# Moving all SSM input products, the second gates and the second time step into the first stage of a conv–Mamba block

## The chip, the cores and the metric

The kernel runs on one core of a Trainium2 chip. The metric is device time in microseconds (us) for one execution of the whole program. Of the kernel before there are three timed runs, and one profiled execution whose trace is read here. The engines are named as in the profile: PE multiplies matrices, DVE, ACT and POOL work on rows of 128 partitions, and SP issues the DMA transfers, in order, from one queue.

## The reference, cut to what matters

One block works on 1024 tokens of width 1024, all in fp32. Cut to the lines that the change touches or that stand beside it:

```
shift, scale, gate = adaln(c, w_ada_mix, b_ada_mix)        # mod = silu(c) @ w + b, 3 x 1024
h    = rms_norm(x, norm_mix_w) * (1 + scale) + shift
proj = h @ w_in
conv_in, z, xbc, dt_raw, g_conv, g_ssm = split(proj, [2048, 2048, 3072, 32, 1024, 1024])
u      = a_half * sigmoid(b_half)                           # conv_in
u      = silu(layer_norm(causal_depthwise_conv31(u)))       # mean and variance over 1024 channels
y_conv = u @ w_conv_out
xbc    = silu(causal_depthwise_conv4(xbc))                  # xs: 2048, B: 512, C: 512 channels
dt     = softplus(dt_raw + dt_bias)
y      = ssd_chunked_scan(xs, dt, -exp(a_log), B, C) + d_skip * xs
y      = group_rms_norm(y * silu(z)) * ssm_norm_w           # 4 groups of 512 channels
y_ssm  = y @ w_ssm_out
x      = x + gate * ((sigmoid(g_conv) * y_conv + sigmoid(g_ssm) * y_ssm) @ w_out)
# then a SwiGLU FFN with its own adaln (w_ada_ffn), and a final rms_norm
```

## The kernel before, in words

The activations stand transposed: 128 channels on the partitions, 512 tokens along the row. The 1024 tokens are two halves of 512 (`hf` 0 and 1), and a width of 1024 is eight such tiles. Every fp32 value that PE multiplies is split into a rounded part and a rest (`h` and `l` in the names), and one product of a 128x128 weight block with a 128x512 tile is three matmuls: high by high, high by low, low by high. All of these are called wide matmuls below.

There are two ways to compute a product of `h` with columns of `w_in`. A plain one, `mm3` (L177), takes one 128-column chunk and one half of the tokens: eight blocks by three matmuls, 24 wide matmuls. It needs the whole chunk split (128x1024, `split_w_`, L163 on ACT and L164 on DVE), and it needs that again for the other half. The other way is a unit (`Unit`, L904), which takes two chunks and both halves at once and uses a scheme of seven block products in place of eight: 7 x 12 = 84 wide matmuls where four plain products take 96. A unit combines quarters of the raw weights (L928 to L937), splits seven sums of them (`wsplit`, L795 and L796), and leaves its results in three PSUM tiles, uX, uY and uZ. Its operands for the second half are differences of the two halves' tiles, T1 to T4 and B22, made once by `tok_ops`.

**First stage** (`phase_a`). After the first norm and six plain gate products (`gate0`), 27 units run, one every 84 matmuls: eight for `conv_in`, eight for z, five for the gates and six (`SsmIn`) for the SSM inputs of groups 0 and 3 (`G_BOTH`). The list `CI_AT` and the insertions by `G_AT` and `G_STEP` set their order. The width-4 convolution of an SSM chunk follows inside its unit, in two halves of 512 tokens, with three more small instructions for the seam (L1131). From the fifth unit on POOL makes the weight sums and splits (`ENG_A`). Background generators are drained by `tick` at a set number of steps per 12 matmuls (`set_drains`): here the width-31 convolution (`conv31`, 47 steps on DVE for each 128 channels), its mean (`conv_mean`), the variance of the first half (`conv_var(0)`), and the time step of the first half (`dt_part`).

**Second stage** (`phase_b`). Plain products follow for groups 1 and 2, half by half: `group` with `conv4`, 24 chunk halves, and `gates1`, six products of the second half. `next_h` makes the normed second half for them from x (it is written to `O`). Beside these run the products with `w_conv_out` (`conv_out`), `w_ssm_out` (`smul`) and `w_out` (`wout`), 1536 wide matmuls together. In the background run the scan (`ssd_all`, which waits for `ready` and for the time step), the second half's time step, `conv_norm` and `conv_var(1)`, and the modulations: `ada` multiplies 128x512 pieces of `w_ada_mix` and `w_ada_ffn` with silu(c) on DVE (L249).

The scan takes eight groups in a row, (half, g). One group turns B over (`bT`, L510), makes C·B (`cb`) and the masked `cbm`, turns the inputs over (`xT`), makes the four chunk states (`st`, L536), and then for four pairs of heads loads rows of the decays from DRAM (M, L547, and E, L603), lets ACT and DVE make M of them, multiplies (`yo`, L608, and `yd`, L623) and gates with z (`y`, L629). `ssd_norm` then sends a row of group norms through DRAM (`bcy`), scales y (L652) and stores it. The y tiles are a ring of four, the M tiles too. `ysplit` loads y back as an operand of `smul` and waits for its group.

**Third stage**: the FFN (`ffn_in`, `down_both`, `down_rest`), which the change leaves alone.

The order on each engine is not the written one. The framework orders the instructions of every engine by a model of their times, under the dependences and with a preference for weight loads (`PRI_W`). Each engine then runs its list in order, so that an instruction which waits holds up those behind it; that is true of SP's list too.

## Time and profile before

| | |
|---|---|
| three timed runs, median (lowest to highest) | 2091.88 us (2086.75 to 2101.56) |
| the profiled execution: its own time | 2084.13 us |
| its span, first to last instruction | 2082.4 us |
| busy: PE, DVE, ACT, POOL | 1941.3, 1574.0, 1004.0, 646.8 us |
| moved by DMA | 366.43 MB, mean 176 GB/s |

The profile lists busy time per engine and per group of instructions; a line such as L164 is a line of the kernel before. A matmul that is followed at once by another counts from its start to its modelled end, so the sum over single matmuls is larger than the time that they take up. A group's row gives its count, its busy time and the mean of one instruction, and then the idle time of the engine just before these instructions and what ended it. A row by window gives for a stretch of time each engine's busy time and count, the granted PE clock, the share of the 16 DMA engines and the GB/s.

### The profile page before, as it was taken

To read this page: it belongs to the slowest core of one execution; us is meant where nothing else is said; L and a number is where in the kernel's file an instruction comes from. 1 tells how busy PE (TensorE), PEld (TensorE's weight loads), DVE (VectorE), ACT (ScalarE), POOL (GpSimd) and SP (SyncE) were. 2 spreads that over 40 slices of the span, in tenths; PEclk is the share of its full clock that TensorE was granted. 3 is DMA by queue.
4 is the path that set the end of the run, shared out by engine and by line. 5 is a ranking of instruction groups with operands and counts; after the bars stand their busy time and mean duration, and the time that the engine had idled before them with its cause. 6 is when DMAs were issued, how large, how long until landed. Compare 5 with 4: busy or idle time off the path is not lost.

```text
span 2082.4 us, 26179 instructions
## 1 busy us (share of the span) xinstructions
PE 1941.3 (93%) x8802; PEld 1548.7 (74%) x8802; DVE 1574.0 (76%) x2458; ACT 1004.0 (48%) x1938; POOL 646.8 (31%) x487
## 2 busy tenths in 40 slices
PE   4899899999998899998899999998999999989997
PEld 3788688887876677776677777776888888767876
DVE  8878989878797978989797965759543443699655
ACT  4644454443444867566555733335333333444243
POOL 0008688888870000100000000005443443331400
...
GB/s 348 86 105 93 76 97 102 116 86 107 104 86 215 271 198 237 243 294 304 266 315 264 239 247 245 250 241 64 154 81 86 85 73 101 186 244 234 202 174 119
DMA packets 163958, 366.43 MB, mean 176 GB/s; under 512 B 18744, under 2 KB 19184, under 8 KB 163824
## 3 DMA queue, kind: packets, MB, share of 16 engines
...
q14 instruction: 65, 0.53, 0.1%
...
## 4 chain that ended last, share of the span: by engine, by line
PE 59%; DVE 20%; DMA 12%; issue 4%; ACT 3%; POOL 1%; SPq 0%; DVEq 0%; ACTq 0%; POOLq 0%
PE uXp L817 10%; PE uXf L817 10%; PE uZp L817 5%; PE uZf L817 5%; PE uXd L817 3%; PE uYp L817 2%; PE uYf L817 2%; DMA M<-acs_d 2%; PE s L189 2%; PE s L187 2%; PE s L188 2%; DMA E<-eac_d 2%; DMA wa_f<-in 1%; DVE gc L1128 1%; DMA wa_m<-in 1%
## 5 line engine op out<-in xcount | busy, mean ns | idle before, releaser
L163 ACT ACTIVATE wh<-w 128x1024 fp32r<-128x1024 f32 (+1 forms) x110 | 113.4, 1032 | 108.6 <-PE s L188 37.4
L164 DVE TENSOR_TENSOR wl<-w,wh 128x1024 fp32r<-128x1024 f32 (+1 forms) x110 | 130.7, 1189 | 23.3 <-ACT wh L163 15.8
L531 POOL TENSOR_TENSOR S<-S,dt_etot 128x512 f32<-128x512 f32 x16 | 20.5, 1281 | 294.7 <-ACT S L538 138.5
L557 ACT ACTIVATE M<-M,dt_acs 128x128 f32<-128x128 f32 x256 | 80.0, 394 | 59.4 <-DMA M<-acs_d 58.6
L930 POOL TENSOR_TENSOR fw<-fw,fw 128x512 f32<-128x512 f32 x37 | 59.5, 1608 | 120.2 <-DMA fw<-in 118.6
L672 DVE SCALAR_TENSOR_TENSOR pcM<-u,cw_eo,pcM 128x512 f32<-128x512 f32 x120 | 90.2, 752 | 2.5
L672 DVE SCALAR_TENSOR_TENSOR pcQ<-u,pc,pcQ 128x512 f32<-128x512 f32 x112 | 84.3, 753 | 2.7
L187 PE MATMUL s<-Hh,wh 128*128 128x512 f32 x192 | 76.4, 402 | 6.3 <-ACT Hh L217 4.0
L672 DVE SCALAR_TENSOR_TENSOR pcR<-u,pc,pcR 128x512 f32<-128x512 f32 x104 | 78.4, 754 | 2.7
L189 PE MATMUL s<-Hh,wl 128*128 128x512 f32 x192 | 76.8, 400 | 3.6 <-DVE wl L164 3.6
L187 PE MATMUL p<-Hh,wh 128*128 128x512 f32 x144 | 62.3, 453 | 18.0 <-DVE xo L1109 9.0
L188 PE MATMUL s<-Hl,wh 128*128 128x512 f32 x192 | 77.1, 402 | 0.9 <-DVE Hl L218 0.8
L845 POOL TENSOR_TENSOR b<-Hh,Hl 128x512 f32<-128x512 f32 x4 | 5.9, 1480 | 223.3 <-DVE spare L329 211.9
L817 PE MATMUL uXp<-T2h,dp 128*128 128x512 f32 x216 | 72.0, 395 | 3.0 <-ACT dp L795 3.0
L817 PE MATMUL uZp<-B22h,ep 128*128 128x512 f32 x216 | 72.4, 397 | 2.2 <-POOL ep L796 1.6
L817 PE MATMUL uYp<-Hh,bp 128*128 128x512 f32 x216 | 72.8, 399 | 1.0 <-DVE s1g L997 1.0
L817 PE MATMUL uXp<-T3h,fp 128*128 128x512 f32 x216 | 72.0, 396 | 1.2 <-ACT s L985 0.9
L817 PE MATMUL uXp<-T4h,gp 128*128 128x512 f32 x216 | 72.5, 396 | 0.4 <-DVE s5c L997 0.4
L817 PE MATMUL uZp<-T1h,cp 128*128 128x512 f32 x216 | 72.0, 395 | 0.0
L817 PE MATMUL uXp<-Hh,ap 128*128 128x512 f32 x216 | 71.0, 390 | 0.0
L188 PE MATMUL p<-Hl,wh 128*128 128x512 f32 x144 | 61.3, 427 | 5.4 <-DVE Hl L346 5.4
L817 PE MATMUL uZf<-T1h,cf 128*128 128x512 f32 x176 | 59.4, 401 | 3.5 <-DVE g L997 3.5
...
## 6 DMA issues: line engine op xcount, KB each, us to landing
fw<-in SPq DMA_DIRECT2D x134, 512.0 KB, 3.3
w<-in SPq DMA_DIRECT2D x100, 512.0 KB, 5.1
...
```

What stands on the lines that cost most here:

```text
L163: act(out=hi, in_=w[:, :nk * P], func=AF.Copy)
L164: eng.tensor_tensor(out=lo, in0=w[:, :nk * P], in1=hi.bitcast(F32), op=ALU.subtract)
L187: nc.tensor.matmul(out=out, lhsT=whi[:, sl], rhs=rh, start=first and i == 0, stop=False)
L188: nc.tensor.matmul(out=out, lhsT=whi[:, sl], rhs=rl, start=False, stop=False)
L189: nc.tensor.matmul(out=out, lhsT=wlo[:, sl], rhs=rh, start=False, stop=last and i == n - 1)
L531: gp.tensor_tensor(out=v3(sn), in0=v3(S[c]), in1=heads(etot, c, g), op=ALU.mult)
L557: act(out=m[:, sl], in_=m[:, sl], func=AF.Relu, scale=-1.0, bias=acs[:, c * 32 + hd:c * 32 + hd + 1])
L672: vec.scalar_tensor_tensor(out=pt if k < n - 1 else out or pt, in0=src(k), scalar=w(k), in1=pt, op0=ALU.mult, op1=ALU.add)
L817: nc.tensor.matmul(out=out, lhsT=l[:, sl], rhs=r, start=first and k == 0 and i == 0, stop=k == 3 and i == 2, skip_group_check=True)
L845: gp.tensor_tensor(out=t, in0=H[k][0].bitcast(F32), in1=H[k][1].bitcast(F32), op=ALU.add)
L930: e[8].tensor_tensor(out=a21, in0=a11, in1=a21, op=ALU.subtract)
L1128: vec.scalar_tensor_tensor(out=t[:, d:], in0=src[:, :T - d], scalar=wc(k), in1=t[:, d:], op0=ALU.mult, op1=ALU.add)
```

## The change

All twelve `SsmIn` units (four groups) now stand in the first stage, which has 33 units in place of 27; `S_AT` lists their places. The width-4 convolution runs over both halves at once, on rows of 1024 tokens, when both are there, so the seam's small instructions go and three DVE instructions per chunk are left; `conv4`, `group`, `next_h` for the second half and the list `ready` are gone. The second half of the six first gates (`gates1`, 24 matmuls each) becomes `gate1` and `half_b`, placed after the units in `GATE_AT`, with 24 matmuls each on the operands B22 and T3 that the units have already. The time step of the second half is made in the same way from those operands (`dt_part(1)`, started by `conv_mean`). The variance of the second half (`conv_var(1)`) and nearly all the modulations (`ada_bg`) are drained in the first stage too. The last two units of the first stage are kept for the end (`A_TAIL`), and ahead of them `tail` starts the layer norm of the first half, `conv_norm(0, H)`.

The second stage starts the scan at once and has only `conv_out`, `smul` and `wout` beside it, in a new order (both halves of `conv_out` first). The scan's input tiles get twice the buffers (`N_BC`, `N_XS`), and a group's inputs are loaded while the group before is at step `SSD_AHEAD`. In all there are 72 wide matmuls fewer, and 30 fewer splits of whole weight chunks.

```
-G_BOTH = (0, 3)
-G_AT, G_STEP = 3, 4
+A_TAIL = 2
+S_AT = (4, 7, 10, 13, 15, 17, 20, 23, 25, 27, 29, 31)
+GATE_AT = (5, 8, 11, 14, 18, 21)
-CONV_RATE = 2.2
+CONV_RATE = 2.4
-SSD_RATE = 0.85
+SSD_RATE = 1.2
-ADA_RATE = 0.6
-MEAN_WAIT = 10
+ADA_RATE = 0.75
+N_BC, N_XS = 4, 8
+SSD_AHEAD = 16
+MEAN_WAIT = 24
+N_EV = 4
...
+    def half_b(out, raw, name):
+        a, b = raw
+        s = pools["u"].tile([P, T], F32, tag="fs", name="fs" + name, bufs=pools["nfs"])
+        gp.tensor_tensor(out=s, in0=a, in1=b, op=ALU.add)
+        mmp(out, wsplit(s, "s" + name, vec), BO["B22"])
+        t = w2("n" + name)
+        hi, lo = t[:, 0:4 * P], t[:, 4 * P:]
+        act(out=hi, in_=a, func=AF.Copy, scale=-1.0)
+        vec.scalar_tensor_tensor(out=lo, in0=a, scalar=-1.0, in1=hi.bitcast(F32), op0=ALU.mult, op1=ALU.subtract)
+        mmp(out, (hi, lo), BO["T3"], False)
...
             if self.i == KD - 1:
-                bg_conv_a.extend([conv_mean(), conv_var(0)])
+                bg_conv_a.extend([conv_mean(), conv_var(0), conv_var(1)])
...
     class SsmIn(Sums):
-        def conv(self, src, m, hf, before=None):
+        def conv(self, src, m):
...
-            t = mp.tile([P, T], F32, tag="x0", name=f"gc{hf}_{i}", bufs=2)
+            t = mp.tile([P, 2 * T], F32, tag="x2", name=f"gc{i}", bufs=2)
             act(out=t, in_=src, func=AF.Identity, scale=wc(SW - 1), bias=sb_h[:, i:i + 1])
             for k in range(SW - 1):
                 d = SW - 1 - k
-                vec.scalar_tensor_tensor(out=t[:, d:], in0=src[:, :T - d], scalar=wc(k), in1=t[:, d:],
+                vec.scalar_tensor_tensor(out=t[:, d:], in0=src[:, :2 * T - d], scalar=wc(k), in1=t[:, d:],
                                          op0=ALU.mult, op1=ALU.add)
-                if before is not None:
-                    vec.scalar_tensor_tensor(out=t[:, :d], in0=before[:, T - d:], scalar=wc(k), in1=t[:, :d],
-                                             op0=ALU.mult, op1=ALU.add)
...
+        def tail(_):
+            finish(bg_dt)
+            bg_conv_a.append(conv_norm(0, H))
...
-        for n, (g, q) in enumerate((g, q) for g in (1, 2) for q in range(6)):
-            group(0, g, H, [q])
-            if 0 <= n - NH_AT < KD:
-                next_h(n - NH_AT, O, r_x[1], "x1m", lambda k: xT[1, :, k, :], gmix, mod_m)
-        step(spares)
-        conv_to(0, H)
-        gates1()
-        group(1, 1, O)
         step(lambda _: conv_done(0))
         many(lambda m: conv_out(0, m, H), range(KD))
+        step(lambda _: conv_done(1))
+        many(lambda m: conv_out(1, m, O), range(6))
         ysplit(0, 0, H)
-        group(1, 2, O)
+        many(lambda m: conv_out(1, m, O), range(6, KD))
         many(lambda m: smul(0, 0, m, H, None), range(KD))
```

How the lists of the engines change is shown at three places. The first is DVE's list in the first stage, where an SSM unit has its convolution. `gc` is the convolution's result, `gx` and `s` are the two halves of its input before (`gx` holds both after), `pcR` and `pcQ` are running sums of the width-31 convolution, and `s1z` and `gy` are results of units. Before:

```order
L1128 SCALAR_TENSOR_TENSOR gc_16_1621<-s_1601,pc,gc_16_1621 128x509
L1131 SCALAR_TENSOR_TENSOR gc_16_1621<-gx_1367,pc,gc_16_1621 128x3
L672 SCALAR_TENSOR_TENSOR pcR_1521<-u_1219,pc,pcR_1521 128x512
L997 TENSOR_TENSOR s_1581<-s_1581,uXp_1350 128x512
L1128 SCALAR_TENSOR_TENSOR gc_16_1621<-s_1601,pc,gc_16_1621 128x510
L1131 SCALAR_TENSOR_TENSOR gc_16_1621<-gx_1367,pc,gc_16_1621 128x2
```

And now, later in the same stage; `ud` and `sav` belong to a variance, `wa_f` and `gffn` to the modulations:

```order
L1151 SCALAR_TENSOR_TENSOR gc_5572<-gx_5292,pc,gc_5572 128x1021
L1032 TENSOR_TENSOR gy_5519<-gy_5519,uXp_5272 128x512
L332 TENSOR_TENSOR sav_5464<-sav_5464,sqv_3_5549 128x512
L1151 SCALAR_TENSOR_TENSOR gc_5572<-gx_5292,pc,gc_5572 128x1022
L744 TENSOR_TENSOR ud_4_5553<-ud_4_5553,bcmean_5440 128x512
L1151 SCALAR_TENSOR_TENSOR gc_5572<-gx_5292,pc,gc_5572 128x1023
L252 ISA wa_f_01_5557,gffn<-wa_f_01_5557,rw,as_f_0_5555 128x512
```

The convolution's instructions are twice as long and have no seam, and variances and modulations stand between them which came in the second stage before.

The second place is PE's list where the first stage ends. `uXp` is the last unit, `p_10` the first plain product of group 1, `co_0` the first product with `w_conv_out`, whose operands H are the layer norm's output. Before:

```order
L817 MATMUL uXp_4784<-T4h_1039,gp_5058 128x512
L188 MATMUL p_10_5138<-Hl_116,wh_5130 128x512
L189 MATMUL p_10_5138<-Hh_115,wl_5131 128x512
L187 MATMUL p_10_5138<-Hh_117,wh_5130 128x512
L188 MATMUL p_10_5138<-Hl_118,wh_5130 128x512
```

And now:

```order
L191 MATMUL co_0_6595<-Hl_112,wh_6587 128x512
L192 MATMUL co_0_6595<-Hh_111,wl_6588 128x512
L190 MATMUL co_0_6595<-Hh_113,wh_6587 128x512
L191 MATMUL co_0_6595<-Hl_114,wh_6587 128x512
L192 MATMUL co_0_6595<-Hh_113,wl_6588 128x512
L840 MATMUL uXp_6128<-T4h_1022,gp_6536 128x512
L840 MATMUL uXp_6128<-T4l_1023,gp_6536 128x512
```

Six of the eight tiles of the layer norm are now used before the last block product of the last unit.

The third place is PE's list inside the first group of the scan; `p_20` is a plain product of group 2, `S` the chunk states, `wx` and `btok` what they are made of, `bc` the tile of C. Before:

```order
L187 MATMUL p_20_5692<-Hh_117,wh_5609 128x512
L536 MATMUL st_5381<-wx_5339,btok_5177 128x512
L292 MATMUL bx1m<-ident,r_x_129 4x128
L188 MATMUL p_20_5692<-Hl_118,wh_5609 128x512
L189 MATMUL p_20_5692<-Hh_117,wl_5610 128x512
L608 MATMUL yo_5458<-bc_20_5156,S_5250 128x128
L608 MATMUL yo_5458<-bc_20_5156,S_5321 128x128
L536 MATMUL st_5462<-wx_5384,btok_5177 128x512
```

And now:

```order
L551 MATMUL st_6798<-wx_6745,btok_6630 128x512
L623 MATMUL yo_6840<-bc_20_6601,S_6694 128x128
L623 MATMUL yo_6840<-bc_20_6601,S_6725 128x128
L190 MATMUL co_5_7085<-Hh_117,wh_6996 128x512
L191 MATMUL co_5_7085<-Hl_118,wh_6996 128x512
L192 MATMUL co_5_7085<-Hh_117,wl_6997 128x512
L551 MATMUL st_6844<-wx_6801,btok_6630 128x512
```

The filler between the scan's steps is now products with `w_conv_out`, no longer products whose result needs a convolution. Counted in wide matmuls without the states, PE's list has 2407 from the first `uXp` to the first `bT`, 1435 from there to the last `yd` of the scan, 730 from there to the first matmul of the FFN and 2808 after it; now these are 3034, 968, 498 and 2808. Between the same two ends of the scan SP's list had transfers of 141 MB, counted from the first `xs` to the last E, and now has 104 MB.

213 lines of the change are left out of this document (94 added, 119 removed).

## The prediction

> **What bounds the kernel now.** I read the page first, then busy time by window over the four stretches that the order of PE's work gives, then the scan group by group, and last DVE's groups of instructions in two of the stretches. In the page's first part stand busy time, share of the span and count per engine:
>
> ```profile
> span 2082.4 us, 26179 instructions
> PE 1941.3 (93%) x8802; PEld 1548.7 (74%) x8802; DVE 1574.0 (76%) x2458; ACT 1004.0 (48%) x1938; POOL 646.8 (31%) x487
> ```
>
> PE is busy nearly throughout, but an average over stages hides where it runs freely and where it is held up. The next rows are windows: the start, the first stage up to the first step of the scan (`bT`), a piece of that stage, the scan up to the last group's end, the rest of the second stage, and the FFN. Columns: length, then busy time of PE, PEld, DVE, ACT and POOL with counts, the granted PE clock, the DMA share, GB/s.
>
> ```profile
> 0.00:65.80 65.80, 35.43 (x129) 26.86 (x129) 54.04 (x110) 34.09 (x55) 1.60 (x10) 0.95 0.78 289
> 65.80:669.80 604.00, 578.49 (x2473) 463.38 (x2474) 519.37 (x731) 278.10 (x469) 384.20 (x301) 0.98 0.31 104
> 300.00:400.00 100.00, 99.64 (x431) 80.52 (x430) 94.22 (x124) 44.52 (x76) 84.51 (x68) 1.00 0.30 103
> 669.80:1209.00 539.20, 493.50 (x2597) 383.12 (x2596) 465.08 (x847) 352.43 (x866) 31.15 (x32) 0.96 0.82 263
> 1209.00:1384.70 175.70, 170.93 (x728) 137.79 (x728) 108.90 (x176) 60.12 (x82) 1.29 (x1) 0.98 0.73 242
> 1384.70:2082.40 697.70, 662.90 (x2881) 537.57 (x2879) 426.63 (x595) 279.26 (x467) 228.54 (x143) 0.98 0.43 143
> ```
>
> In the middle of the first stage (300 to 400) PE has no gap: 431 matmuls in 100 us, 0.232 us each, although DVE is busy 94% and POOL 85%. So there PE is the bound, and a busy DVE does not hold it up. During the scan it is otherwise. PE is busy 91.5% (493.5 of 539.2), at a lower clock, and its list has only 1435 wide matmuls, 333 us at 0.232, beside the scan's own small ones. These are the eight groups of the scan, from one `bT` to the next:
>
> ```profile
> 669.81:731.44 61.63, 52.41 (x279) 40.68 (x278) 54.09 (x84) 50.71 (x134) 3.68 (x8) 0.92 0.85 278
> 731.44:836.36 104.92, 98.50 (x476) 74.34 (x474) 87.06 (x176) 70.11 (x159) 3.37 (x6) 0.95 0.70 216
> 836.36:888.93 52.57, 52.57 (x282) 41.46 (x281) 47.36 (x88) 30.72 (x86) 5.41 (x3) 1.00 0.79 255
> 888.93:978.51 89.58, 81.49 (x417) 63.99 (x417) 78.34 (x143) 59.94 (x146) 5.39 (x4) 0.96 0.89 293
> 978.51:1022.54 44.03, 42.27 (x256) 33.69 (x254) 35.26 (x77) 22.60 (x61) 3.13 (x3) 1.00 0.76 254
> 1022.54:1076.50 53.96, 45.10 (x245) 33.29 (x245) 45.62 (x84) 35.32 (x96) 3.13 (x3) 0.94 0.96 317
> 1076.50:1146.95 70.45, 65.95 (x350) 52.15 (x349) 59.51 (x104) 38.36 (x91) 4.58 (x3) 0.98 0.88 279
> 1146.95:1209.00 62.05, 55.19 (x302) 43.52 (x301) 57.84 (x98) 44.68 (x100) 2.48 (x2) 0.95 0.74 235
> ```
>
> A group's length follows the work put beside it: 44 us where that is least, 105 us where it is most. DVE is busy 80 to 93% of each group and close to PE in all. The two together set the pace, and what stands beside the scan decides how long it takes.
>
> **The change, part by part.** The start and the FFN keep their lists: 65.8 us and 697.7 us stay.
>
> *First stage.* Its list grows from 2407 to 3034 wide matmuls, by 627: six units of 84, the gates' 144, the time step's 24 and 22 of `conv_out` come in, 67 of plain products go. At 0.232 us (the row 300 to 400) that is 145.5 us, and the stage goes from 604.0 to 749.5 us if PE stays the bound. DVE's part has to be shown to fit. These rows are the width-4 convolution (L1128, and the seam L1131) between 65.8 and 580, and then L1128 after 612, with shortest, median and longest:
>
> ```profile
> L1128 DVE SCALAR_TENSOR_TENSOR gc<-s,pc,gc 128x509 f32<-128x509 f32 (+2 forms) x21 | 22.4, 1066 | 0.0
> L1128 DVE SCALAR_TENSOR_TENSOR gc<-gx,pc,gc 128x509 f32<-128x509 f32 (+2 forms) x12 | 15.8, 1317 | 1.0 <-ACT gc L1125 0.9
> L1131 DVE SCALAR_TENSOR_TENSOR gc<-gx,pc,gc 128x3 f32<-128x3 f32 (+2 forms) x12 | 10.6, 885 | 0.0
> L1128 DVE SCALAR_TENSOR_TENSOR gc<-gy,pc,gc 128x509 f32<-128x509 f32 (+2 forms) x9 | 8.9, 991 | 0.0
> L1131 DVE SCALAR_TENSOR_TENSOR gc<-gy,pc,gc 128x3 f32<-128x3 f32 (+2 forms) x9 | 4.0, 439 | 0.0
> ...
> L1128 DVE SCALAR_TENSOR_TENSOR gc<-s,pc,gc x12: 737/741/751, 614.5 to 656.5; 128x509 f32<-128x509 f32 x4, 128x510 f32<-128x510 f32 x4, 128x511 f32<-128x511 f32 x4
> ```
>
> And two rows of the scan's window, where POOL is all but idle, the split of a whole weight chunk and a modulation piece:
>
> ```profile
> L164 DVE TENSOR_TENSOR wl<-w,wh 128x1024 fp32r<-128x1024 f32 x60 | 74.0, 1234 | 8.3 <-ACT wh L163 8.3
> ...
> L249 DVE CUSTOM_DVE_ANT_0 wa_f<-wa_f,rw,as_f 128x512 f32<-128x512 f32 x16 | 12.4, 778 | 5.2 <-DMA wa_f<-in 5.2
> ```
>
> After 612 one instruction takes 0.741 us; while POOL splits weights it takes 1.12 us (47.1 over 42). Even the seam's rows of one to three elements mean 0.885 us. So what is lost beside POOL looks like a wait per instruction, 0.38 us on these, not a slower pace. The new instructions have twice the length. None is in this trace; the nearest is the 1024-wide two-input split, L164, at 1.234 us. With one wait of 0.38 that is 1.61 us, and 72 of them 116 us; without any wait they cost 89 us, and stretched in proportion (1.12 over 0.741) 134 us. I take 116, for the short rows' sake.
>
> The Trainium skill (SBUF — State Buffer, section "Who interferes with whom") says that a DVE instruction with two SBUF inputs and a POOL instruction that reads SBUF exclude each other for the whole instruction, and that the later one is blocked, not slowed. The short rows agree. By that rule the 116 us stand; by a shared bandwidth it would be the 134.
>
> The old convolution cost 61.7 us in the five rows up to 580, and some 22 more until 670 (ten of the 24 chunk halves at three times 0.741), so the new one adds 32 us. With the other work that comes in, DVE gains: 18 additions of unit results at about 0.7, 12; 48 modulation pieces at 0.778 (L249) and a wait of 0.38, 56; parts of the variances, 19 at 0.7, 13; three quarters of one layer norm, 18 at 0.7, 13; twelve gate splits, 9; a second time step, 15 by my estimate from some 20 instructions of 0.7; and it loses about 15 of plain products. Together 135 us: 654 of 749.5, 87%, where it has 86% now and bears 94% in the row 300 to 400 with PE full. POOL gains 72 instructions at 1.24 (84.51 over 68), 89 us: 63%, as now. For longer waits of SP behind the convolution's stores, and for the end, where the layer norm has to be ready before PE's last unit is through, I add 5 us, between 0 and 40. The cover of all this is PE's list; what it costs without it is the second rival.
>
> *The scan.* It loses 467 wide matmuls beside it, 108.3 us at 0.232; of PE's 493.5 us 385.2 are left. On DVE these rows of the scan's window matter too:
>
> ```profile
> L1106 DVE SCALAR_TENSOR_TENSOR p<-pre,pc,p 128x512 f32<-128x512 f32 x63 | 46.8, 750 | 0.3 <-ACT p L1102 0.2
> ...
> L652 DVE SCALAR_TENSOR_TENSOR y<-y,pc,bcy 128x512 f32<-128x512 f32 x28 | 19.2, 748 | 6.6 <-DMA bcy<-row_d 6.6
> ...
> L1109 DVE SCALAR_TENSOR_TENSOR xo<-pre,p 128x512 f32<-128x512 f32 x22 | 15.0, 682 | 4.2 <-DMA xbc_d<-xo 2.5 <-ACT pre L1108 1.6
> ...
> L746 DVE SCALAR_TENSOR_TENSOR un<-lnt,un 128x512 f32<-128x512 f32 x16 | 11.4, 715 | 0.9 <-ACT lnt L741 0.9
> ...
> L721 DVE TENSOR_TENSOR ud<-ud,bcmean 128x512 f32<-128x512 f32 x10 | 6.8, 687 | 2.0 <-DMA ud<-uc_d 2.0
> ```
>
> `conv4` goes (46.8 + 15.0), 19 of 60 weight splits (19 x 1.234 = 23.4), all 48 modulation pieces that ran here (48 x 0.778 = 37.3), 30 of 48 layer norm steps (21.5), the variance (6.8), and `next_h` (16 at 0.75, 12.0). That is 162.8; 13 more pieces of `conv_out` and y splits come in (8.9). DVE keeps 311 of 465 us. At the fullest group's share (57.84 of 62.05, 93%) it needs 334 us, at today's 86% 361. ACT's 352 us now are below that before anything is taken off. SP's list carries 104 MB in place of 141, which over 393 us is the 263 GB/s of now, within 1%. So PE is the later one: 385 us, at the share it has in the two groups with little DVE work (52.57 of 52.57 and 42.27 of 44.03, 98% in the mean) 393 us, 49 a group. At today's 91.5% it is 421; with a full clock and no gap 370 (385 x 0.96). I take 393, by those two groups, since these have what all have now: products and scan, little beside. The waits that go are those of `group` for its convolution; what is late next is a pair of M tiles or the y ring.
>
> *The rest of the second stage.* It has 498 wide matmuls in place of 730; at 175.7/730 = 0.241 us each, 119.9 us.
>
> The sum is 65.8 + 749.5 + 5 + 393 + 119.9 + 697.7 = 2030.9 us, and with the 1.7 us between span and time 2032.6 against the profiled 2084.1, 2.5% less. The median of the three runs lies 0.37% above the profiled one; I carry that over: 2040 us against 2091.9. Of the 51.5 us, 72 x 0.232 = 16.7 are fewer matmuls and the rest is the scan no longer held up.
>
> **The rivals.**
>
> *The scan's own chain sets the pace.* A group must load M and E, pass them through ACT and DVE, norm its y by way of DRAM and give its y tiles back before the next group can load z into them. For it: on ACT these waits are the largest of the scan,
>
> ```profile
> ACT M L557 <- DMA M<-acs_d: 58.6, 27, 6.7
> ```
>
> in total, times and longest; L652 waits 6.6 us for `bcy`; and groups one and eight take 61.63 and 62.05 us with only 52 to 55 us of PE work. If each group takes 62 us whatever stands beside it, the scan takes 496, and the time is 2136 by the profile, 2143 by the median. Against it: one group went through in 44.03 us and two more in under 54. It makes the kernel slower from 55.6 us a group on, (393 + 51.5)/8, and by over 1% from 58.2.
>
> *DVE holds up the longer first stage.* If it can't pass today's 86% there and its convolution stretches in proportion, 672 us of work (654 + 18) need 781: 32 us more, in place of the 5 counted, so 2060, or 2067 by the median. With a layer norm that is late at the end as well (40 us) it is 2100 by the profile. For it: its list now has the variances, which go through DRAM twice, among 27 to 33 units. Against it: the row 300 to 400.
>
> *The scan keeps PE's share.* If its gaps come from the scan and not from `conv4`, 385.2/0.915 = 421: 2061, or 2068 by the median, and with a few us more in the first stage no change that can be told.
>
> *Better than forecast.* With PE's clock full throughout the scan, 370, and nothing lost at the end of the first stage, 2005 by the profile, 2012 by the median; with the scan at DVE's 361, 1996 and 2003.
>
> **How the numbers follow.** About 1% is what a measurement of this kernel can tell from no change: 2071 to 2113. The forecast (2012 to 2062 by the median) gets 0.53, the better case 0.13, the scan at PE's present share 0.11, DVE in the first stage 0.09, the scan's chain 0.14. The predicted time is 2040. The range goes from 1996, a little below the better case's 2003, to 2100, which takes in the second and third rival and both together (27 + 28 us on 2040, 2095); it leaves out most of the slow case. Faster by over 1%: the forecast and the better case, 0.66. Within 1%: the second and third rival, 0.20. Slower: the scan's chain, 0.14.
>
> **What would show it.** The first stage is right if the last `uXp` ends near 740 to 790 us with PE at 0.232 us a matmul in mid-stage, and wrong if PE's waits there name DVE or ACT for tens of us. The price of the long convolution: a mean near 1.6 us for the 1021- to 1023-wide rows; 1.9 speaks for a stretch. The scan: eight groups between 44 and 54 us each, first `bT` to last `yd` about 393 us, PE over 95% busy. If groups take 60 us with PE under 85% and the waits name M, `bcy` or y, the first rival is right. The whole is wrong if the FFN's 697.7 us change, since nothing in it does.

## The result and the profile after

The changed kernel takes 2102.9 us in the median of 20 runs (2092.3 to 2119.7), the kernel before on the same chips 2089.4 (2084.9 to 2101.6). The ratio is 1.0063, with a 95% interval of 1.0042 to 1.0083: slower by 0.6%, where 2.5% less was forecast. The profiled execution took 2103.7 us, close to the median.

The first part of its page shows PE with 4.5 us less to do than before, in a span that is 19.3 us longer:

```profile
span 2101.7 us, 25836 instructions
PE 1936.8 (92%) x8729; PEld 1541.7 (73%) x8729; DVE 1551.6 (74%) x2312; ACT 993.3 (47%) x1885; POOL 777.9 (37%) x547
```

The next rows are the windows of the prediction: start, first stage up to the first `bT`, a piece of that stage, scan, rest of the second stage, FFN (columns as there).

```profile
0.00:68.80 68.80, 36.12 (x128) 27.52 (x128) 59.16 (x126) 34.34 (x55) 1.53 (x8) 0.90 0.83 308
68.80:850.70 781.90, 738.54 (x3161) 589.12 (x3161) 659.64 (x906) 370.91 (x594) 514.55 (x371) 0.97 0.39 129
300.00:400.00 100.00, 98.82 (x430) 80.07 (x429) 90.34 (x111) 42.25 (x70) 86.36 (x66) 1.00 0.29 93
850.70:1268.00 417.30, 376.27 (x2059) 290.80 (x2058) 314.63 (x536) 262.63 (x704) 29.66 (x24) 0.94 0.77 250
1268.00:1403.00 135.00, 122.46 (x507) 95.70 (x506) 90.12 (x152) 46.02 (x66) 1.29 (x1) 0.95 0.72 242
1403.00:2101.70 698.70, 663.39 (x2881) 538.53 (x2879) 428.03 (x595) 279.44 (x467) 230.91 (x143) 0.98 0.43 143
```

Against the forecast's 2030.9 us the difference of 70.8 lies so: start +3.0, first stage +27.4 (781.9 against 749.5 + 5), scan +24.3 (417.3 against 393), rest +15.1 (135.0 against 119.9), FFN +1.0. The middle of the first stage (300 to 400) runs as freely as before.

The eight groups of the scan, `bT` to `bT`, the last to its last `yd`:

```profile
850.69:898.65 47.96, 47.96 (x259) 37.48 (x257) 36.30 (x54) 36.46 (x95) 3.52 (x3) 1.00 0.97 336
898.65:950.88 52.23, 44.34 (x230) 32.73 (x229) 33.98 (x62) 30.72 (x88) 3.54 (x3) 0.87 0.63 199
950.88:1000.29 49.41, 43.63 (x250) 34.08 (x250) 39.71 (x69) 32.20 (x92) 4.33 (x3) 0.93 0.80 266
1000.29:1051.72 51.43, 45.29 (x234) 34.08 (x233) 34.05 (x60) 33.14 (x92) 5.11 (x4) 0.93 0.68 218
1051.72:1100.26 48.54, 39.99 (x232) 31.32 (x231) 34.95 (x63) 31.45 (x87) 3.13 (x3) 0.83 0.88 281
1100.26:1165.69 65.43, 59.26 (x304) 46.19 (x303) 53.61 (x89) 34.71 (x84) 4.82 (x3) 0.97 0.77 243
1165.69:1221.72 56.03, 52.52 (x288) 40.64 (x287) 44.16 (x75) 34.06 (x90) 3.13 (x3) 0.97 0.81 262
1221.72:1268.00 46.28, 43.27 (x269) 34.28 (x269) 37.87 (x72) 29.90 (x80) 2.09 (x2) 1.00 0.63 199
```

They are closer to one another than before, 46 to 65 us long and 52.2 in the mean. PE is busy 90.2% of the scan and DVE only 75% (86% before), so neither is full. These are the two waits of the scan that the prediction watched, for M and for `bcy`, and the largest two of PE (total us, times, longest):

```profile
ACT M L572 <- DMA M<-acs_d: 63.3, 25, 8.8
DVE y L667 <- DMA bcy<-row_d: 17.9, 7, 3.8
...
PE yd L638 <- DVE M L577: 13.2, 4, 6.7
PE st L551 <- ACT wx L596: 12.9, 5, 7.4
```

Last, two stretches of the first stage in which PE isn't full, near its start and at its end, and then the end of that stage in the kernel before:

```profile
100.00:150.00 50.00, 36.14 (x131) 27.90 (x130) 42.30 (x91) 23.40 (x41) 0.25 (x2) 0.80 0.48 152
...
700.00:850.70 150.70, 129.13 (x528) 98.71 (x527) 121.14 (x152) 84.26 (x133) 72.21 (x48) 0.93 0.55 178
```

```profile
600.00:669.80 69.80, 55.40 (x220) 42.65 (x219) 58.65 (x86) 32.41 (x55) 20.20 (x17) 0.90 0.47 157
```

Before, PE was busy 48.84 us between 100 and 150. What is new there are the modulations' pieces. They are written across the first stage, but their loads depend on nothing but a free buffer, and the ordering of SP's list has put 36 of the 48 between 60 and 160 us, three ahead of that and five right behind, among the building of the token operands T1 to T4 on DVE.

### The profile page after: what moved, and what is told of

It reads as the page before. It is cut to its first block, busy times and chain, and to the rows that moved or that the text cites. A ratio compares the mean times of both kernels' runs of the same rounds, so it can differ in the third digit from the quotient of the medians.

```text
span 2101.7 us, 25836 instructions
## 1 busy us (share of the span) xinstructions
PE 1936.8 (92%) x8729; PEld 1541.7 (73%) x8729; DVE 1551.6 (74%) x2312; ACT 993.3 (47%) x1885; POOL 777.9 (37%) x547
## 4 chain that ended last, share of the span: by engine, by line
PE 55%; DVE 19%; DMA 14%; issue 4%; POOL 3%; ACT 3%; SPq 1%; DVEq 0%; ACTq 0%; POOLq 0%
PE uXp L840 10%; PE uXf L840 9%; PE uZp L840 5%; PE uZf L840 4%; PE uXd L840 3%; PE uYp L840 2%; PE uYf L840 2%; PE s L190 1%; PE s L192 1%; PE s L191 1%; PE uZd L840 1%; DVE gc L1151 1%; DMA yl<-y_d 1%; DMA M<-acs_d 1%; DMA fw<-in 1%
## 5 line engine op out<-in xcount | busy, mean ns | idle before, releaser
L166 ACT ACTIVATE wh<-w 128x1024 fp32r<-128x1024 f32 (+1 forms) x80 | 82.0, 1027 | 73.3 <-PE s L191 29.4
L167 DVE TENSOR_TENSOR wl<-w,wh 128x1024 fp32r<-128x1024 f32 (+1 forms) x80 | 94.6, 1182 | 27.2 <-ACT wh L166 21.6
L840 PE MATMUL uXp<-T2h,dp 128*128 128x512 f32 x264 | 90.2, 404 | 11.7 <-ACT cg L1009 6.1
L840 PE MATMUL uXp<-T4h,gp 128*128 128x512 f32 x264 | 90.7, 405 | 1.8 <-DVE gy L1032 1.7
L840 PE MATMUL uZp<-T1h,cp 128*128 128x512 f32 x264 | 89.3, 400 | 2.9 <-ACT cp L818 2.9
L819 POOL TENSOR_TENSOR ap<-fw,ap 128x512 fp32r<-128x512 f32 x29 | 41.5, 1430 | 84.0 <-ACT ap L818 83.9
L840 PEld LDWEIGHTS uXp<-T2h,dp 128*128 128x128 f32 x264 | 50.7, 193 | 24.2 <-ACT cg L1009 6.5
L868 POOL TENSOR_TENSOR b<-Hh,Hl 128x512 f32<-128x512 f32 x4 | 5.9, 1484 | 166.7 <-DVE spare L332 155.4
L960 POOL TENSOR_TENSOR fw<-fw 128x512 f32<-128x512 f32 x43 | 62.3, 1450 | 2.0
L840 PEld LDWEIGHTS uZp<-B22h,ep 128*128 128x128 f32 x264 | 50.7, 192 | 16.4 <-ACT gy L1160 2.5
L840 PEld LDWEIGHTS uXp<-T4h,gp 128*128 128x128 f32 x264 | 51.2, 194 | 15.7 <-DVE gy L1032 3.1
```

The lines of the kernel that those rows point to most:

```text
L166: act(out=hi, in_=w[:, :nk * P], func=AF.Copy)
L167: eng.tensor_tensor(out=lo, in0=w[:, :nk * P], in1=hi.bitcast(F32), op=ALU.subtract)
L819: eng.tensor_tensor(out=lo, in0=raw, in1=hi.bitcast(F32), op=ALU.subtract)
L840: nc.tensor.matmul(out=out, lhsT=l[:, sl], rhs=r, start=first and k == 0 and i == 0, stop=k == 3 and i == 2, skip_group_check=True)
L960: e[10].tensor_tensor(out=a12, in0=a12, in1=a11, op=ALU.subtract)
```

## The experiments

Ratios are to the kernel before, with 95% intervals; that of the changed kernel is 1.0063. Stages are from one profiled execution each, while executions of the changed kernel alone lie up to 27 us apart, so a few us in a single stage decide nothing; the scan goes to its last `yd`, 416.6 us in the changed kernel by that count, and a point in time at which the scan starts also moves with the conv_out products done ahead of it.

| run | median us | ratio to before | first stage | scan | rest |
|---|---|---|---|---|---|
| changed kernel | 2102.9 | 1.0063 (1.0042 to 1.0083) | 781.9 | 416.6 | 135.7 |
| modulations late | 2123.2 | 1.0159 (1.0133 to 1.0185) | 777.6 | 438.6 | 135.6 |
| modulations in the second stage | 2127.5 | 1.0179 (1.0158 to 1.0200) | 773.7 | 449.3 | 138.8 |
| modulations spread | 2113.4 | 1.0125 (1.0108 to 1.0141) | 798.6 | 418.4 | 134.5 |
| conv_out(1) behind | 2133.9 | 1.0198 (1.0173 to 1.0224) | 780.3 | 415.4 | 166.7 |
| thin products (one run) | 2093.0 | | 777.0 | 405.7 | 139.3 |
| scan rate 1.5 | 2080.0 | 0.9971 (0.9952 to 0.9990) | 792.4 | 386.0 | 146.0 |
| scan rate 4 | 2125.3 | 1.0171 (1.0151 to 1.0191) | 785.2 | 372.1 | 201.4 |
| M ahead | 2089.2 | 1.0004 (0.9986 to 1.0021) | 780.0 | 412.1 | 132.7 |
| M ahead, rate 1.5 | 2087.3 | 0.9990 (0.9969 to 1.0011) | 778.5 | 385.5 | 147.5 |
| M ahead, rate 2.0 | 2089.4 | 1.0022 (0.9998 to 1.0046) | 780.6 | 391.8 | 151.3 |
| stores off SP | 2097.6 | 1.0047 (1.0027 to 1.0067) | 784.1 | 412.2 | 134.8 |
| stores off SP, M ahead, rate 1.5 | 2100.2 | 1.0066 (1.0041 to 1.0090) | 779.4 | 407.2 | 145.3 |
| no z loads | 2083.5 | 0.9984 (0.9963 to 1.0004) | 778.8 | 399.5 | 135.0 |
| z loads twice | 2113.0 | 1.0115 (1.0096 to 1.0134) | 782.4 | 421.1 | 136.3 |
| long convolutions faster | 2107.6 | 1.0107 (1.0072 to 1.0142) | 789.3 | 413.2 | 135.1 |
| mean earlier | 2104.8 | 1.0092 (1.0066 to 1.0119) | 804.2 | 395.4 | 134.4 |
| spread, rate 1.5 | 2096.7 | 1.0049 (1.0033 to 1.0064) | 798.9 | 381.2 | 146.9 |
| time step 1 in the middle, rate 1.5 | 2095.0 | 1.0032 (1.0013 to 1.0052) | 790.0 | 387.0 | 147.1 |

**What sets the scan's length.** First, products were moved out of it, and then most of their matmuls were taken away.

```
-            bg_conv.append(conv_norm(1, O))
...
+        step(lambda _: bg_conv.append(conv_norm(1, H)))
+        many(lambda m: wout(0, m, O), range(KD))
+        step(lambda _: conv_done(1))
+        many(lambda m: conv_out(1, m, H), range(4))
+        ysplit(1, 0, O)
+        many(lambda m: conv_out(1, m, H), range(4, KD))
```

> Edit: the second half's convolution product (192 matmuls of 128x512) and the layer norm ahead of it stand again behind the first half's output product, as in the kernel before, so that they lie beside the last groups of the scan and behind it; nothing is left out. Theory W (the scan lasts as long as the products beside it, at 90% of PE): the scan shrinks by about 192 x 0.232 / 0.9 = 49 us, to 365 to 380; the rest behind it grows from 135 by 37 to 45 us, less than was taken, because the last group's hand-over has products again; the whole 2093 to 2103. Theory C (the scan lasts as long as its own chain of loads, exponentials and products, about 50 us a group): the scan stays at 405 to 425, the rest grows to 172 to 180, the whole 2130 to 2150.

```
-                mm3(pt, w, W8, ops)
+                mm3(pt, w, [0], ops)
+                for _ in range(4):
+                    tick()
```

> Edit: of the 24 matmuls of each of the 16 convolution output products 21 are left out (336 matmuls, 78 us of PE), their loads, evictions and stores stay; this leaves out part of the computation. It measures what the scan takes by itself. Theory W (the products beside it set the scan's length): the scan falls from 417 to 330 to 350 us. Theory C (its own chain, 50 us a group): the scan stays above 395 us. Between the two (part of the groups are bound by the chain): 350 to 395, and the groups that have no product beside them show the chain's own length.

With `conv_out(1)` moved behind, the scan stays at 415.4 us and the rest grows by 31. The other run leaves out 336 matmuls, 78 us of PE's work; 279 of them, 65 us at 0.232, lay in the scan. It still takes 405.7 us, and PE simply stands more. The scan's windows of the two runs, in this order:

```profile
849.70:1265.00 415.30, 352.71 (x1878) 267.47 (x1876) 305.41 (x515) 255.90 (x697) 29.28 (x24) 0.88 0.74 234
```

```profile
845.90:1251.60 405.70, 327.55 (x1778) 245.20 (x1777) 315.45 (x535) 262.12 (x704) 33.84 (x24) 0.88 0.78 257
```

So the forecast's measure, PE's work over PE's share, doesn't give the scan's length: for the second of them it would have made it 327.55/0.98 = 334. The first also shows what the stretch behind the scan lacks. With `conv_out(1)` placed there, PE has something to do during the last group's hand-over:

```profile
1265.00:1431.80 166.80, 159.38 (x688) 128.44 (x687) 107.89 (x177) 58.03 (x79) 1.29 (x1) 0.99 0.74 245
```

PE is busy 95.6% there, 90.7% in the changed kernel, at 0.242 us a matmul against 0.266: the forecast's 0.241 was right for a tail that has products left.

Then the scan's steps were put first, at other rates:

```
-SSD_RATE = 1.2
+SSD_RATE = 1.5      # and 4
```

> Edit: the scan's steps are put among the products at 1.5 instead of 1.2 for each tick, so that fewer product matmuls lie within a group; nothing is left out. Theory C (the scan's own chain sets its length, 50 us a group): the scan gets no shorter than 400 us, the products left over lie behind it, and the whole grows by 5 to 25 us. Theory W (the products beside it set it): the scan falls by about a fifth, to 335 to 350, the rest grows by as much, the whole within 5 us of 2103.

> Edit: from the changed kernel, the scan's steps at 4 a tick instead of 1.2, so that the scan has almost no products among it and these lie behind it; nothing is left out. It measures how long a group takes by itself. VectorE's work of the scan alone is about 214 us and ScalarE's 200 (sums of their groups of instructions in the changed kernel's scan). If a group has a chain of its own of 45 to 50 us: scan 360 to 400, the whole 2160 to 2200. If it has not, and only the products queued between its steps stretch it: scan 240 to 300, the whole 2090 to 2120.

The groups of the run at 4, where products only fill what the scan leaves:

```profile
853.91:896.74 42.83, 42.83 (x235) 33.22 (x234) 29.55 (x42) 30.84 (x84) 3.24 (x3) 1.00 0.96 324
896.74:937.76 41.02, 26.20 (x165) 19.13 (x164) 30.33 (x56) 27.70 (x86) 3.58 (x3) 0.81 0.65 213
937.76:981.74 43.98, 26.38 (x147) 19.22 (x145) 31.36 (x59) 29.91 (x93) 3.52 (x3) 0.77 0.57 186
981.74:1022.01 40.27, 27.29 (x146) 20.30 (x146) 29.95 (x57) 26.11 (x80) 4.19 (x4) 0.71 0.63 185
1022.01:1079.32 57.31, 48.85 (x254) 37.29 (x253) 43.16 (x72) 35.98 (x101) 3.13 (x3) 0.89 0.80 252
1079.32:1127.25 47.93, 44.26 (x258) 34.08 (x256) 37.39 (x66) 28.53 (x71) 3.13 (x3) 1.00 0.76 246
1127.25:1171.34 44.09, 43.18 (x257) 34.14 (x258) 31.96 (x55) 29.14 (x80) 3.35 (x3) 1.00 0.72 227
1171.34:1226.00 54.66, 50.97 (x281) 39.77 (x279) 46.09 (x80) 30.08 (x80) 2.48 (x2) 0.97 0.80 262
```

Three groups, the second to the fourth, have PE busy only 60 to 68%, at a granted clock of 0.71 to 0.81, and DVE and ACT below 75%, and still take 40 to 44 us. That is about a group's own length, with hardly a product beside it (one group of the run with `conv_out(1)` behind took 36.5 us, with 34 product matmuls beside it). The other five, with products beside them, take 43 to 57 us. All eight make 372 us, 46 in the mean, which neither 1.2 steps a tick (417) nor 1.5 (386) reaches. The theory of the chain holds for the scan of this run; the whole, 2125, is below what it gave (2160 to 2200), and PE is busy 95% of the time behind the scan. Rate 1.5 fits neither of its expectations. The theory of the chain had a scan of no less than 400 us and a longer whole, the theory of the products a scan of 335 to 350 us, and the scan took 386 with the whole shorter. It fell by 31 us with only 98 matmuls (23 us) moved out, and these lie behind it where they were missing:

```profile
861.10:1247.10 386.00, 350.12 (x1959) 267.86 (x1957) 304.86 (x515) 253.30 (x692) 28.41 (x24) 0.95 0.80 260
1247.10:1393.10 146.00, 141.02 (x606) 113.53 (x607) 102.79 (x172) 54.44 (x78) 1.30 (x1) 0.98 0.76 252
```

Scan and rest together take 532.0 us in place of 552.3. The first stage took 10.5 us more in this execution, with 3160 matmuls against 3161 and nothing edited in it; about 8 us of that lie between 450 and 550 us, where PE does 386 matmuls in place of 421, and why is open. The profiled execution was the slowest of that run, 2093.3 against a median of 2080.0, so the gain in the median is larger than in the trace. At 2080.0 us it is the fastest kernel here, 0.9% below the changed kernel and 0.3% below the one before.

So the 52 us of a group in the changed kernel are neither PE's work nor a group's own length of about 40 us alone. The scan gets shorter when fewer steps of products are queued among its own (417, 386 and 372 us at the three rates), and hardly when only their matmuls are left out (406), or when `conv_out(1)` stands behind it (415). In that last run the scan has 179 matmuls fewer, the products of some seven steps, so their number alone doesn't decide either. Which part of a product's step stretches a group, its weight splits, evictions and loads or its place in the lists that the engines run in order, no run here shows.

**What a group's length consists of.** Edits to the M tiles, to SP's list and to the bytes took away one suspect each, all of them at rate 1.2 first. The M tiles:

```
-N_BC, N_XS = 4, 8
+N_BC, N_XS = 4, 6
...
-                    m = sp.tile([P, T], F32, tag="M", name=f"M{hf}{hd}", bufs=4)
+                    m = sp.tile([P, T], F32, tag="M", name=f"M{hf}{hd}", bufs=6)
...
-        M = Decay(0)
+        Ms = [Decay(j) for j in range(4)]
+        M = Ms[0]
...
             elif c == 1:
+                Ms[1].load()
                 M.exp(0)
...
-            if j < 3:
-                M = Decay(j + 1)
-                M.load()
+            if j < 2:
+                Ms[j + 2].load()
+            if j < 3:
+                M = Ms[j + 1]
```

> Edit: the decay tiles M get six buffers instead of four, and each pair is loaded one step of the group earlier; two buffers of xs are given up for the room; nothing is left out. Measured so far: with 78 us of product matmuls left out the scan still took 405.7 of 416.6 us, so that something in the scan itself sets its length, about 50 us a group. Theory M (that is the round of an M buffer: store free, load of 5.8 us, exponentials, product, matmul): the wait of ACT's L572 for M's loads falls from 63 us to under 20, the scan from 417 to 375 to 395, the whole from 2103 to 2065 to 2085. Rival D (the in-order work of DVE, ACT and PE on one another, M's load only the last of several equal waits): ACT's wait for M falls, others take its place, the scan stays at 408 to 420, the whole 2095 to 2106.

The whole, 2089.2, lies between the two expectations: 0.6% gained. But the scan of the profiled run is only 4.5 us shorter and ACT's wait for M is 54.4 us still; the rest of the gain is spread over all stages in pieces of 2 to 3 us and can't be put in one place. Two runs had it together with the scan's steps at a higher rate:

```
-SSD_RATE = 1.2
+SSD_RATE = 1.5      # and 2.0, both with M as above
```

> Edit: both together, M with six buffers and its loads a step earlier (alone: 2089 us), and the scan's steps at 1.5 a tick (alone: 2080 us); nothing is left out. If the two take time from different waits (M's loads in the one, too many product steps queued between two steps of the scan in the other), their gains of 14 and 23 us against 2103 add: 2063 to 2072. If both shorten the same round of the scan, the second adds nothing to the first: 2076 to 2084.

> Edit: as the run before, with the scan's steps at 2.0 a tick instead of 1.5; nothing is left out. If a group's own chain of about 46 us is what is left, the scan stays at 360 to 385 us, products are left over behind it and the whole is 2080 to 2095. If the scan's length goes with the number of product steps queued between its own, it falls to 310 to 340 us, the rest grows by 50 to 60, and the whole is 2060 to 2075.

The first is above both of its expectations: the two gains do not add, and with the rate at 1.5 the earlier M loads bring nothing. At 2.0 the scan takes 392 us, above the 360 to 385 of its first expectation. But its window has the same 1994 matmuls as at 1.5, so the higher rate took no products out of the scan, and the run decides less than it was meant to.

Next came SP's list:

```
-                    dma(out=sp_d[hf, m], in_=t)
+                    nc.scalar.dma_start(out=sp_d[hf, m], in_=t)
...
-                dma(out=mp_d[hf, m], in_=t)
+                gp.dma_start(out=mp_d[hf, m], in_=t)
...
-                dma(out=x1_d[hf, m], in_=xt)
+                gp.dma_start(out=x1_d[hf, m], in_=xt)
```

> Edit: from the changed kernel, the stores of the second part's products are issued by other engines than SP: the first half products sp by ScalarE, the convolution's products mp and the residual x1 by GpSimd; nothing is left out. In the changed kernel's scan SP's queue stood 29 us for gcl, 24 us for sp and 14 us for xr, and what is queued behind (M, E, xs, weights) went out later. Theory Q (that in-order queue makes the scan's loads late): the scan falls from 417 to 380 to 402, the whole from 2103 to 2070 to 2090. Theory V (the bytes: 104 MB at 250 to 263 GB/s in every version so far) and the theory of the group's own chain of 46 us: the scan stays at 406 to 422, the whole 2095 to 2108.

SP's largest waits in the scan, in the changed kernel and then in this run:

```profile
SPq L1295 <- DVE gcl L1294: 29.1, 5, 16.5
SPq L1305 <- ACT sp L1304: 24.3, 6, 11.1
SPq L155 <- DVE wl L167: 21.3, 14, 4.2
```

```profile
SPq L155 <- DVE wl L167: 72.6, 20, 17.7
```

The two waits are gone and the weights' buffer (L155) has taken their place: SP stands at the next thing in its list that isn't ready. All its waits in the scan's window add up to 249 us in the changed kernel and to 252 in this run. The scan is 4 us shorter, and the whole can't be told from the changed kernel (the intervals overlap). So moving these stores doesn't help; whether a queue that stands less would help isn't tested by it, since this one stands as long as before. With all three edits the kernel is 0.8% slower than with the other two alone (1.0066 against 0.9990), and above both expectations:

> Edit: the stores of the product steps off SP, M with six buffers and earlier loads, the scan's steps at 1.5 a tick, together; nothing is left out. The last two together gave 2087. Theory Q: the loads that are written earlier now also go out earlier, ScalarE's wait for M falls from 62 us to under 35, the scan is 345 to 370, the whole 2058 to 2074. Theories V and of the chain: the scan 378 to 392, the whole 2078 to 2092.

Last, the bytes, once fewer and once more:

```
-            dma(out=y, in_=z_d[hf, g * 4 + j])
+            gp.memset(y, 1.0)
```

> Edit: from the changed kernel, the scan's 32 loads of z (256 KB each, 8.4 of 104 MB) are left out; GpSimd fills their tiles with a constant instead, so the gate z is left out of the computation. Theory V (the scan moves its bytes at about 250 GB/s and lasts as long as they do): 95.7 MB, the scan 375 to 390 us, the whole 2065 to 2080. Theories Q and of the chain (M's round is not touched, z is loaded well ahead): the scan 405 to 420, the whole 2093 to 2106.

```
             dma(out=y, in_=z_d[hf, g * 4 + j])
+            xtra = sp.tile([P, T], F32, tag="xtra", name=f"xtra{hf}{g}{j}", bufs=1)
+            dma(out=xtra, in_=z_d[hf, g * 4 + j])
```

> Edit: from the changed kernel, each of the scan's 32 loads of z is done a second time, into a tile that nobody reads; nothing is left out. 8.4 MB come on top of 104, 33.5 us of DMA at 250 GB/s, and no work on any other engine than SP's issue. Theory V2 (bytes beside the scan cost about half their time, as the scan without z loads gave 17 us back): the scan 428 to 440 us in place of 417, the whole 2115 to 2127. Rival Y (that run was faster since a z load has to wait for its y tile and nothing waited for it any more, not since there were fewer bytes): the scan 412 to 424, the whole 2098 to 2110.

Without z the scan is 17 us shorter, and its 399.5 us and the whole's 2083.5 lie between the two expectations; with z twice it is 4.5 longer in the profile, and the whole 0.5% slower, some 10 us by the median. The scan's window of the latter, and ACT's wait for M in it:

```profile
851.80:1272.90 421.10, 376.81 (x2071) 288.81 (x2070) 317.86 (x539) 262.61 (x704) 28.12 (x24) 0.94 0.83 268
```

```profile
ACT M L572 <- DMA M<-acs_d: 90.4, 25, 12.6
```

It moves 268 GB/s, so 250 was no ceiling; 8.4 MB more, 33.5 us of DMA at 250 GB/s, cost 5 to 10 us. M came later (90 us of waiting in place of 63) and the scan got only 4.5 us longer, so at this rate most of the added wait for M is slack. The whole of that run, 2113.0, lies between its two expectations. That the run without z gained more than the bytes alone explain fits what the rival says, that a z load waits for its y tile; it isn't shown which part is which. So none of the loads, stores and buffers tried at rate 1.2 brings the scan down to what it takes at rate 4; they move it by 4 to 17 us, and 4 us in one profile can't be told from none. None of them was tried at rate 4, where a group stands nearly alone. The trace of that run names a suspect: in the chain of what released what, followed back through its three groups with hardly a product (896.74 to 1022.01 us), loads of M take 23.5% of the time, loads of `bcy` 8.8%, ACT's steps on `wx` and M 6.5 and 6.1%, and nothing else over 6%. In the scan of the changed kernel loads of M take 6.7% of that chain. Whether earlier M loads would shorten a group that stands alone, no run shows.

**The modulations.** Three edits moved the 48 pieces that the change had moved (16 more stand in the rest of the second stage in both kernels): 30 of them into the scan, all into the second stage as before the change, and spread over the first stage by an order on SP.

```
-            bg_ada.append(late(30, ada_bg()))
+            bg_ada.append(late(150, ada_bg()))
```

> Edit: the generator of the modulations' pieces waits 150 instead of 30 steps, so that most of its 48 pieces of x 128x512 are put behind the last units of the first stage and into the scan; nothing is left out. Theory A (the pieces that ran among the building of the token operands cost the first stage its lost time between 60 and 150 us): the stretch 100 to 150 us goes from 36.1 us of PE's busy time back to 46 or more, the first stage falls from 781.9 to 762 to 768 us, and the whole from 2103 to 2083 to 2092. Rival B (the early loss comes from the order of the units and their weights, the pieces only fill gaps there): 100 to 150 stays at 36 to 39, the first stage within 5 us of 781.9. Rival C (the pieces cost the same wherever they lie): the first stage falls by 14 to 20 us, and the scan or the rest behind it grows by as much; the whole stays within 5 us of 2103.

```
-            bg_ada.append(late(30, ada_bg()))
...
-            yield from ada(None, wada_mix, range(8, 12), mod_m, gmix, "m")
+            yield from ada(pools["b"], wada_mix, range(8, 12), mod_m, gmix, "m")
...
-        set_drains((bg_ssd, SSD_RATE), (bg_conv, CONV_RATE_B), (bg_ada, 1))
+        set_drains((bg_ssd, SSD_RATE), (bg_conv, CONV_RATE_B), (bg_ada, ADA_RATE))
...
+            bg_ada.append(ada_bg())
```

> Edit: one part of the change is undone: the modulations' pieces stand again in the second stage, at 0.75 pieces a step from its first step, with a buffer of their own; nothing is left out. Theory A (their place among the building of the operands is what costs): first stage 762 to 768 us, 100 to 150 at 46 us of PE or more, scan no longer than 422, the whole 2083 to 2092. Rival B: first stage within 5 us of 781.9, the whole 2098 to 2108. Rival C: first stage 762 to 768, scan and rest together 14 to 20 us longer than their 552, the whole within 5 us of 2103.

```
-                        dma(out=w, in_=wada[2 * b + m, :, q * T:(q + 1) * T])
+                        # last_store[0]: the last store of gate_out or SsmIn.conv
+                        with tc.issue_after(last_store[0]) if last_store[0] else nullcontext():
+                            dma(out=w, in_=wada[2 * b + m, :, q * T:(q + 1) * T])
```

> Edit: from the changed kernel, each modulation piece's load is ordered on SP behind the last store of a gate or an SSM row written ahead of it, so that the 48 pieces lie where the program has them, across the first stage, and no longer go ahead of it into 60 to 130 us; nothing is left out. Theory A2 (pieces among the operand building cost 10 to 13 us there: 36.1 us of PE in 100 to 150 against 46.0 and 49.3 with the pieces moved away; spread out they cost nothing): 100 to 150 at 45 or more, the first stage 766 to 774 us, the scan as it was, the whole 2088 to 2096. Rival D2 (VectorE, busy 88 to 90 of 100 us between 150 and 350, has no room for them, and what depends on it comes late by as much): 100 to 150 at 45 or more but the first stage 778 to 786, the whole 2098 to 2108.

Between 100 and 150 us PE's busy time comes back in each; this is the row of the run with them in the second stage:

```profile
100.00:150.00 50.00, 49.25 (x205) 40.26 (x206) 39.41 (x62) 21.66 (x38) 0.42 (x1) 0.94 0.29 96
```

So their place does cost 10 to 13 us there. But of that the first stage keeps 4 and 8 us, and the scan grows by 22 and 33: rival C's place, at more than its price. The scan, whose DVE has a quarter of its time free, pays for the pieces (36 us of DVE and 12.6 MB for all 48) almost as if it were full. In these two scans DVE stands 15 and 28 us for the loads of the pieces; that this belongs to the price is likely, but isn't shown. Spread out, they lengthen the first stage by 17 us, more than either expectation of that run had. Two groups of the pieces in the first stage of that run come first, then two groups of the changed kernel over its whole span, where most of them run while POOL has nothing to do:

```profile
L254 DVE CUSTOM_DVE_ANT_0 wa_f<-wa_f,rw,as_f 128x512 f32<-128x512 f32 x16 | 19.8, 1239 | 8.2 <-DMA wa_f<-in 8.1
L254 DVE CUSTOM_DVE_ANT_0 wa_m<-wa_m,rw,pc 128x512 f32<-128x512 f32 x8 | 10.2, 1280 | 3.0 <-DMA wa_m<-in 3.0
```

```profile
L252 DVE CUSTOM_DVE_ANT_0 wa_f<-wa_f,rw,pc 128x512 f32<-128x512 f32 x16 | 12.0, 748 | 4.5 <-DMA wa_f<-in 4.4
L252 DVE CUSTOM_DVE_ANT_0 wa_m<-wa_m,rw,as_m 128x512 f32<-128x512 f32 x8 | 6.0, 746 | 0.4 <-DMA wa_m<-in 0.2
```

The 48 pieces take 1.23 us each in the mean beside POOL's splits (59.1 us in all, the shortest 0.73 and the longest 1.88) and 0.75 without. The Trainium skill (SBUF — State Buffer, "Who interferes with whom") has a lock of this kind: a DVE instruction with two SBUF inputs and a POOL one that reads SBUF exclude each other. The trace agrees, with 0.48 us more for each piece, 23 us for the 48, by which DVE's busy time in that stage grew too (659.6 to 683.1). Of the four places the one that the order chose by itself is the cheapest. With the scan's steps at 1.5 the spread pieces cost about as much (0.8%; 0.6% at 1.2), and the whole is above both expectations:

```
-SSD_RATE = 1.2
+SSD_RATE = 1.5      # and the order on SP as above
```

> Edit: as the run before, with the scan's steps at 1.5 a tick instead of 1.2 (alone: 2080 us); nothing is left out. A2: the two gains lie in different stages and add: 2066 to 2074. D2: 2078 to 2086.

**The end of the first stage.** PE stands 21.6 of the last 150.7 us (in the kernel before 14.4 of its last 69.8). Two edits made the layer norm earlier, `CONV_RATE` from 2.4 to 2.7 and `MEAN_WAIT` from 24 to 10, and one put the second half's time step into the middle of the stage, with the scan at 1.5:

```
-CONV_RATE = 2.4
+CONV_RATE = 2.7
```

> Edit: the long convolutions are put into the first stage at 2.7 instead of 2.4 steps for each tick of the products, so that they and the layer norm behind them end earlier; nothing is left out. Between 700 and 850.7 us TensorE was busy 129 of 151 us. Theory L (the layer norm comes late for the first output products, and PE's waits there are its chain): the stretch from 700 us to the scan loses 8 to 15 us, the whole 2088 to 2095. Rival S (PE's waits there come from several short chains, of time steps, weights and evictions, that stand there whenever the layer norm comes): the first stage within 4 us of 781.9, the whole 2098 to 2107.

```
-MEAN_WAIT = 24
+MEAN_WAIT = 10
```

> Edit: the layer norm's mean waits 10 instead of 24 steps behind the last long convolution (the long convolutions keep their pace); nothing is left out. Theory L: the first stage loses 5 to 12 us, the whole 2091 to 2098. Rival S: within 4 us of 2103, and the first stage within 4 us of 781.9.

```
-        bg_dt.append(dt_part(1, lambda n, dt=F32: at.get(n) or ev("dt1" + n, dt)))
...
+        after.setdefault(16, []).append((lambda _: bg_dt.append(dt_part(1, ev)),))
```

> Edit: from the changed kernel with the scan's steps at 1.5 a tick (2080 us), the second half's time steps are computed in the middle of the first stage, with the buffers that the first half's use, and not behind the last long convolution; nothing is left out. Between 700 and 850 us PE waited 21 us in eleven short waits, 7 to 9 of them in the narrow products (dtv, acs, sc). Theory S (these short chains at the end are what costs): the first stage 6 to 12 us shorter, the whole 2066 to 2075. Rival D2 (VectorE has no more room in the middle of the first stage, as the spread modulations showed): the first stage within 5 us or longer, the whole 2077 to 2090.

None gained anything; the last lost 0.6% against rate 1.5 alone, above both of its expectations. In the first two the first stage got 7 and 22 us longer, which neither expectation had, and in the second of them the scan got 21 us shorter. From 700 us to the scan PE stands 25.6 and 22.8 us in them, no less than before the edits, so an earlier layer norm takes nothing off what PE waits for there. With the time step elsewhere its waits (`dtv`, `acs`) are gone, and others, for a unit's eviction (8.2 us) and a row of sums (5.2), are longer. PE has only 92.3 us between 450 and 550 in that run, but 91.4 in the run with rate 1.5 alone, so what the last edit lost stays open. Rival S holds in its first half, that the waits stand there whenever the layer norm comes; what they could be traded for wasn't found.

## Why the prediction was wrong, point by point

**The sum's base.** Start: 3.0 us more. DVE does 16 instructions more there (126 against 110), and the runs without the pieces ahead have 64.4 and 64.6, so these are the modulations too. The FFN, 698.7 against 697.7, was right.

**First stage, 749.5 + 5; it took 781.9.** The pace of PE in the middle was right (430 matmuls from 300 to 400, before 431), and so was DVE's load: 659.6 us, forecast 654. The price of the long convolution was right to the hundredth:

```profile
L1151 DVE SCALAR_TENSOR_TENSOR gc<-gy,pc,gc 128x1021 f32<-128x1021 f32 (+2 forms) x36 | 58.1, 1614 | 1.3 <-DMA xbc_d<-gc 1.0 <-ACT gc L1148 0.2
L1151 DVE SCALAR_TENSOR_TENSOR gc<-gx,pc,gc 128x1021 f32<-128x1021 f32 (+2 forms) x36 | 57.6, 1601 | 0.0
```

The mean is 0.35 us above the shortest, 1.26. It is a wait and not a stretch: half of the rows in the second line took 1.28 us or less, and the longest 2.33. (Of the seam's two rows the prediction read the one with 0.885 us; the other has 0.439. Nothing rests on it.) What was mis-sized is the hand-over term of 5 us (bounds 0 to 40): it came to 32. Of that 11.1 us is no loss, since 70 wide matmuls of `conv_out` ran ahead of the first `bT` where 22 were counted (48 x 0.232). Of the rest, about 21, one part is the early stretch, where the prediction had 48 modulation pieces hidden under PE's list over the whole stage, and the order put 39 of them ahead of 160 us; the two runs that moved pieces away give back 4 and 8 us in this stage. That could have been read ahead of the forecast: it was in SP's list. Another part is the end of the stage, where PE stands 21.6 us, 7 more than in the kernel before. The last 6 to 10 us stay open. The second rival had 781 us for this stage, and 781.9 came, by luck: it took 672 us of DVE's work at 86% of the time, with a stretched convolution, and DVE had 660 at 84%, without the stretch. And the sign that was set for this stage, the last `uXp` at 740 to 790 us, did not fit the sum, by which the stage ends at 820; it came at 832.

**The scan, 393; it took 417.3.** This is the step that failed most, in its method. PE's work was as forecast (376 us, and 385 less the `conv_out` done ahead), DVE's too (314.6 against 311). But "the later of two engines at 98%" was taken from the two best of eight groups, and the run with 65 us less of PE's work in the scan, which made it only 11 us shorter, shows that PE wasn't the bound at all. The first rival was right that a group has a length of its own, and wrong in its price and in that it doesn't depend on what stands beside it: 62 us came from two long groups, the groups that stand nearly alone at rate 4 take 40 to 44, and the 372 us of that run are below the 393 of the forecast. The changed kernel's 52 us a group come from the group's own steps and the products' steps together; the forecast took the later of the two for the whole. What in the products' steps does it stays open. At 52 us the first rival also stayed under the 55.6 from which it alone would have decided. The third rival gave 421 for the scan, nearly what came. Its premise, that the gaps come from the scan, fits the runs; its price came out by luck, since PE's share of 91.5% doesn't stay: it followed the list down to 81%.

**Rest, 119.9; it took 135.0.** The price of 0.241 us a matmul held where products cover the last group's hand-over (0.242 and 0.241 in two runs) and was 0.266 here, where `conv_out(1)` has been done already. The new order of the products was described and its cover not looked at. PE stands 12.5 us there, where that price has 3.3 (498 times what PE stood before, 4.8 us in 728 matmuls); 2.2 us are nine matmuls more, and what is left of the 15.1 goes with the lower clock (0.95, before 0.98).

**Why slower and not just less fast.** The forecast's gain was 51.5 us by the profile; 3.0 + 27.4 + 24.3 + 15.1 + 1.0 took 70.8. No single rival did it, and what came, within 1% of no change, had 0.20 in the forecast. The modulations' move, which looked like the cheap part, is worth keeping: undone, the kernel is 1.2% slower still.
